# A hybrid encoder block on one core: the four activation block sums of the convolution's fifth product move into PSUM during the last z columns, and the modulation steps of the third z group begin four steps later

## The chip, the cores and the metric

The kernel runs on one core of a Trainium2 chip. Its engines are TensorE (PE in the profile; its weight loads are PEld), VectorE (DVE), ScalarE (ACT), GpSimd (POOL) and SyncE (SP), which here only issues transfers. The metric is the device time of one execution in microseconds; shown is the median of three runs.

## The reference, cut to what matters

One layer of an encoder block over 1024 tokens of width 1024, in float32: a modulation computed from a condition vector, RMSNorm, one input projection, attention, a two-way state-space branch (SSD), a gated merge and an MLP. What the change touches is the modulation and the part of the input projection that makes z and the convolution's input xBC:

```python
mod = jax.nn.silu(c) @ w_ada[l] + b_ada[l]
shift1, scale1, gate1, shift2, scale2, gate2 = [m[:, None, :] for m in jnp.split(mod, 6, axis=-1)]
h = rms_norm(x, norm1_w[l]) * (1.0 + scale1) + shift1
proj = h @ w_in[l]
q, k, v, xBC, z, dt_raw, gates = jnp.split(proj, offsets, axis=-1)
...
xBC = jax.nn.silu(depthwise_conv_centred(xBC, conv_w, conv_b))
```

## The kernel before, in words

A float32 operand is held as two pieces, a high part rounded to the type fp32r and a low part, the rest; a product is three matmuls (high x high, high x low, low x high). `split` makes the pieces: ScalarE copies the high part (line 173, a CAST in the profile), VectorE or GpSimd subtracts for the low part (through the helper `tt`, line 159). The normalised activations `h` lie transposed in SBUF as `hhi` and `hlo` (`hh` and `hl` in the profile), in 8 blocks of 128 features by two halves of 512 tokens.

**z groups.** z is made in four groups of 512 columns by `gemm_tm` (matmuls on lines 518 to 520): eight token tiles a group, each 24 matmuls into one of four PSUM banks `psq`, evicted by ScalarE with a SiLU (line 533) and stored. Each group's weights come in four pieces (`traw`), split into `twh` and `twl`. Beside the third group (`z_run(2, ...)`) runs `mod_stream`, which makes the two gate rows. Each takes eight transfers of 512 KB (`wada`, two buffers, of which the row `grow` takes one at the end), a VectorE multiply-add chain over them into `macc` (lines 224 and 226), and two matmuls with a column of ones (line 549, four rows in the profile), whose result VectorE adds to the bias. `z_run` steps a generator once per quarter of a token tile, 32 times a group; `spaced` passes every second of these on to `mod_stream`. TensorE's order in the third group is the order in which the code is written; the other engines there, and every engine in the fourth group, are put in order by a scheduler that estimates times as it builds the program. Each engine then works through its instructions strictly in that order.

Beside the fourth group (`z_run(3, ...)`) the generator `sums` makes the combinations U3, U2 and U4 of activation blocks that the convolution's products need. GpSimd adds and subtracts in tiles `df` (three buffers), ScalarE and VectorE split the results.

**The convolution's input.** xBC is made in twelve pairs of 128-column blocks, and one more pair for a gate, by Strassen-like recursion (Winograd's form): seven products (`product`, lines 919 to 921, 12 matmuls each, into four PSUM banks `psc`) in place of eight. Their activation operands are H11, H21, U2, U3, U4, H22 and the fifth, T1 = H12 - H11. `first_sum`, called in pair 0 after the second product was added, makes T1 on VectorE in SBUF tiles `u` and writes its two pieces over H12; H12 was stored to DRAM before, and is read back for the last pair. A product's weights are sums of `w_in` blocks made on GpSimd (`ws`), split by ScalarE and by VectorE or GpSimd into `wop`. Each pair's result goes through a five-tap convolution in the PSUM tile `tap` (line 863 on ScalarE, line 865 four times on VectorE, line 868 on ScalarE), and some of it is turned to token order through the PSUM tiles `pst`. tap takes two banks, pst two, psc four; they are allocated together once z's four banks are free. After the convolution come two more gate products (`psg`, line 211) and the attention.

Of the kernel before, what the change touches and what calls it, by code (L numbers as in the profile page):

```python
# [9 lines left out]
F32 = mybir.dt.float32  # L10
# [8 lines left out]
P = 128  # L19
# [72 lines left out]
def block(ctx: ExitStack, tc: tile.TileContext, ia, out, upto=99, dbg=None):  # L92
# [65 lines left out]
    def tt(e, o, a, b, op):  # L158
        e.tensor_tensor(out=o, in0=a, in1=b, op=op)  # L159
# [12 lines left out]
    def split(hi, lo, src, e_hi=None, e_lo=None):  # L172
        (e_hi or A.copy)(hi, src)  # L173
        tt(e_lo or V, lo, src, hi.bitcast(F32), ALU.subtract)
# [627 lines left out]
    with tc.tile_pool(name="p1m", bufs=1, reuse_waits="tile") as p1m, tc.tile_pool(name="ps1m", bufs=1, space=PSUM) as ps1m:  # L802

        mods = mod_stream(p1m, lambda: ps1m.tile([P, 512], F32, name="psm", tag="psm", bufs=2), 1)
        def spaced():
            for n in range(99):
                yield
                next(mods, None)
                yield

        with tc.manual_schedule(engines={mybir.EngineType.PE}):
            first = z_run(2, first, spaced(), 1)
            drain(mods)
# [3 lines left out]
    H11, H12, H21, H22 = ([(hhi[k + j][h], hlo[k + j][h]) for j in range(HK)] for k, h in ((0, 0), (0, 1), (HK, 0), (HK, 1)))  # L817
    U2, U3, U4 = ([tuple(stp.tile([P, 512], F32R, name=f"{n}{q}_{j}") for q in "hl") for j in range(HK)]
                  for n in ("u2", "u3", "u4"))
    with tc.tile_pool(name="p1b", bufs=1, reuse_waits="tile") as p1b:  # L820

        def diff(t, a, b):
            u = p1b.tile([P, 512], F32, name="df", tag="df", bufs=3)
            tt(G, t, a[0].bitcast(F32), b[0].bitcast(F32), ALU.subtract)
            tt(G, u, a[1].bitcast(F32), b[1].bitcast(F32), ALU.subtract)
            tt(G, t, t, u, ALU.add)

        def sums():

            for j in range(HK):  # L830
                t = p1b.tile([P, 512], F32, name="df", tag="df", bufs=3)
                diff(t, H22[j], H12[j])
                split(*U3[j], t)
                yield
                for q in range(2):
                    tt(G, t, t, H11[j][q].bitcast(F32), ALU.add)
                split(*U2[j], t)
                yield
                for q in range(2):
                    tt(G, t, t, H21[j][q].bitcast(F32), ALU.subtract)  # L840
                split(*U4[j], t)
                yield

        todo = sums()
        z_run(3, first, todo, 2)
        drain(todo)
        for j in range(HK):
            for q in range(2):
                dma(h12_d[q][j], H12[j][q].bitcast(F32))
# [4 lines left out]
    with tc.tile_pool(name="p2", bufs=1, reuse_waits="tile") as p2, \  # L854
# [4 lines left out]

        def conv(i, pad):  # L860

            tap = ps2.tile([P, S], F32, name="tap", tag="tap", bufs=1)
            A.activation(tap, pad[:, 0:S], AF.Identity, scale=cwT[:, i:i + 1], bias=vecT[:, CB0 + i:CB0 + i + 1])  # L863
            for k in range(1, 5):
                V.scalar_tensor_tensor(out=tap, in0=pad[:, k:k + S], scalar=cwT[:, 24 * k + i:24 * k + i + 1],  # L865
                                       in1=tap, op0=ALU.mult, op1=ALU.add)
            acc = acc_tile()
            A.activation(acc, tap, AF.Silu)
            if i >= 20:
                adma(bc_d[i - 20][:, 1], acc)  # L870
                return
            if i >= 16:
                adma(bc_d[i - 16][:, 0], acc)
            late.append(lambda: to_tokens(i, acc))
# [1 line left out]
        late = []  # L876

        def to_tokens(i, y):
            st = p2.tile([P, NT, P], F32, name="cst", tag="cst", bufs=2)
            for hf in range(2):  # L880
                pt = ps2.tile([P, 512], F32, name="pst", tag="pst", bufs=2)
                for c in range(4):
                    T.transpose(pt[:, c * P:(c + 1) * P], y[:, (hf * 4 + c) * P:(hf * 4 + c + 1) * P], ident)
                A.copy(st[:, hf * 4:hf * 4 + 4], pt.rearrange("p (c n) -> p c n", c=4))
            if i >= 16:
                adma(xb_d[i - 16][:, :, 512:640], st)
            else:
                adma(xb_d[i // 4][:, :, (i % 4) * P:(i % 4 + 1) * P], st)
# [41 lines left out]
        H0, H1 = slice(2, 514), slice(514, 1026)  # L930
        nxt = load_pair(0)

        tus = [p2.tile([P, 2, 512], F32, name="u1", tag="cst", bufs=2)]
        pre = {"ws": [p2.tile([P, HK, P], F32, name="ws", tag="ws", bufs=4)],
               "c1": [p2.tile([P, 512], F32, name="c1", tag="c1", bufs=2)],
               "p5": [p2.tile([P, 512], F32, name="p5", tag="p5", bufs=1)],
# [6 lines left out]
        def first_sum():  # L943

            for j in range(HK):
                tu = tus.pop() if tus else p2.tile([P, 2, 512], F32, name="u1", tag="cst", bufs=2)
                t, u = tu[:, 0], tu[:, 1]
                tt(V, t, H12[j][0].bitcast(F32), H11[j][0].bitcast(F32), ALU.subtract)
                tt(V, u, H12[j][1].bitcast(F32), H11[j][1].bitcast(F32), ALU.subtract)
                tt(V, t, t, u, ALU.add)  # L950
                split(*H12[j], t)

        for p, (kind, i0, _) in enumerate(pairs):
            r0, r1 = nxt
# [36 lines left out]
            done(kind, i0, pa)  # L991
        while late:
            late.pop(0)()
    sts.close()
    if upto <= 2:
        return dict( z_d=z_d, s2=s2, modc=modc)
# [1052 lines left out]
```

## Time and profile before

| what | value |
|---|---|
| median of three runs | 2447.72 us (2446.38 to 2450.83) |
| the profiled execution | 2451.32 us |
| its span, first to last instruction | 2449.5 us |
| TensorE's mean granted clock | 0.992 |
| TensorE busy, share of the span | 97% |
| HBM read, written | 250.54 MB, 113.84 MB |

In the rows of a timeline stand the start and the length in us, the engine, the line, the operation, what is written and read, and in brackets how long the engine was idle before it and what ended that. Lines are those of the kernel that was run; a helper's line stands for all its callers. Matmuls overlap: the distance between two starts, not the length of a row, is what one costs.

### The profile page before, as it was taken

What the parts mean: (1) busy time and instruction counts of PE and PEld (TensorE: products, weight loads), DVE (VectorE), ACT (ScalarE), POOL (GpSimd) and SP (SyncE); (2) the same over time, 40 slices, a digit from 0 to 9 for tenths busy, and PEclk for the clock granted to TensorE, in tenths of its full rate; (3) what the DMA queues carried; (4) which work ended last, traced back from release to release, by engine and by line L of the source; (5) the groups of instructions that cost most, each with busy time, mean ns of one, the idle gap of its engine ahead of it and who ended that gap; (6) DMA issues with size and microseconds to landing.
All of it is one profiled execution on the core that took longest, in us unless ns stands there. A gap on an engine that the chain in (4) does not pass through costs nothing.

```text
span 2449.5 us, 32244 instructions
## 1 busy us (share of the span) xinstructions
PE 2377.3 (97%) x11307; PEld 1899.4 (78%) x11307; DVE 1702.4 (69%) x2325; ACT 1091.8 (45%) x1884; POOL 827.9 (34%) x637
## 2 busy tenths in 40 slices
PE   8999999999989999999989999999999999999999
PEld 4998877888867777777767767787787888788887
DVE  5876435777756666666577796557568888768794
ACT  5455413555566666666333343344242222364430
POOL 0221107666611111110356666534006786123200
PEclk9999999999999999999999999999999999999999
DMA  7664841333531212111667765476325554654422
GB/s 255 181 184 147 259 167 65 95 104 112 185 112 52 91 52 81 57 54 48 219 205 228 221 208 176 146 270 205 132 74 194 185 197 163 234 171 138 157 79 82
DMA packets 288595, 366.53 MB, mean 150 GB/s; under 512 B 33961, under 2 KB 168849, under 8 KB 288433
## 3 DMA queue, kind: packets, MB, share of 16 engines
q1 hardware_dynamic: 216246, 288.77, 37.2%
q10 hardware_dynamic: 72187, 75.70, 9.3%
q8 instruction: 90, 1.47, 0.2%
q14 instruction: 72, 0.59, 0.1%
HBM read 250.54 MB, written 113.84 MB: 149 GB/s over the span
## 4 chain that ended last, share of the span: by engine, by line
PE 80%; DVE 8%; DMA 5%; issue 2%; ACT 2%; POOL 2%; SPq 0%; ACTq 0%; DVEq 0%; POOLq 0%
PE pst L1059 5%; PE psg L211 4%; PE psg L213 4%; PE psg L212 4%; PE p L1928 3%; PE p L1927 3%; PE p L1926 3%; PE psc L919 3%; PE psc L920 3%; PE psc L921 3%; PE psq L519 3%; PE psq L520 3%; PE psq L518 3%; PE pp L1514 3%; PE pp L1512 3%; PE pp L1513 3%
## 5 line engine op out<-in xcount | busy, mean ns | idle before, releaser
L1046 DVE TENSOR_REDUCE nm<-pss 128x1 f32<-128x1024 f32 x128 | 156.7, 1225 | 125.1 <-PE pss L1044 123.5
L1048 ACT ACTIVATE pf<-pss,nm 128x1024 f32<-128x1024 f32 x128 | 143.0, 1117 | 98.8 <-PE pst L1059 96.1
L159 DVE TENSOR_TENSOR pl<-pst,ph 128x512 fp32r<-128x512 f32 x256 | 167.6, 683 | 27.1 <-ACT ph L173 27.1
L1059 PEld LDWEIGHTS pst<-masks,pf 128*128 128x128 f32 x1024 | 117.8, 140 | 73.8 <-issue 33.9
L519 PE MATMUL psq<-twl,hh 128*128 128x512 f32 (+1 forms) x448 | 168.3, 377 | 2.5 <-DVE twl L159 2.5
L1059 PE MATMUL pst<-masks,pf 128*128 128x128 f32 x1024 | 157.4, 276 | 13.3 <-DVE pl L159 10.8
L173 ACT CAST ph<-pst 128x512 fp32r<-128x512 f32 x256 | 145.9, 586 | 54.5 <-PE pst L1059 37.9
L518 PE MATMUL psq<-twh,hh 128*128 128x512 f32 (+1 forms) x448 | 166.8, 376 | 3.5 <-ACT twh L173 3.5
L520 PE MATMUL psq<-twh,hl 128*128 128x512 f32 (+1 forms) x448 | 167.4, 375 | 0.0
L159 POOL TENSOR_TENSOR av<-av,rz 64x512 f32<-64x512 f32 x32 | 42.0, 1315 | 346.4 <-DMA rz<-rz 141.2
L1926 PE MATMUL p<-o,o 128*128 128x512 f32 x400 | 153.6, 390 | 3.3 <-ACT o L173 1.9
L1927 PE MATMUL p<-o,o 128*128 128x512 f32 x400 | 155.3, 389 | 0.2 <-DVE o L159 0.2
L1928 PE MATMUL p<-o,o 128*128 128x512 f32 x400 | 153.7, 389 | 0.0
L173 ACT CAST wop<-ws 128x512 fp32r<-128x512 f32 x116 | 71.2, 621 | 127.5 <-PE pp L1514 52.4
L865 DVE SCALAR_TENSOR_TENSOR tap<-pad,cwT,tap 128x1024 f32<-128x1024 f32 x96 | 123.4, 1285 | 4.9 <-ACT tap L863 3.5
L159 POOL TENSOR_TENSOR ws<-r,r 128x512 f32<-128x512 f32 x29 | 41.7, 1438 | 215.2 <-DVE ro L159 151.0
L159 POOL TENSOR_TENSOR sl<-sl 128x512 f32<-128x512 f32 x32 | 49.6, 1553 | 179.1 <-DVE o L159 72.7
L173 ACT CAST o<-sl 128x512 fp32r<-128x512 f32 x92 | 56.9, 622 | 104.7 <-PE p L1928 88.7
L1097 PE MATMUL pv<-pl,v 128*64 128x512 f32 x256 | 101.5, 417 | 0.0
L159 DVE TENSOR_TENSOR o<-sl,o 128x512 fp32r<-128x512 f32 x92 | 72.3, 788 | 39.8 <-ACT o L173 39.8
L211 PE MATMUL psg<-hh,whi 128*128 128x512 f32 x224 | 95.3, 425 | 1.2 <-ACT ost L1006 1.2
L518 PEld LDWEIGHTS psq<-twh,hh 128*128 128x128 f32 x448 | 84.8, 189 | 14.6 <-ACT twh L173 3.9
(457 smaller groups left out, 7026.4 us busy)
## 6 DMA issues: line engine op xcount, KB each, us to landing
ar<-r SPq DMA_DIRECT2D x100, 256.0 KB
wada<-in_w_ada_dram SPq DMA_DIRECT2D x48, 512.0 KB
r<-in_w_mlp_dram SPq DMA_DIRECT2D x32, 512.0 KB
sl<-in_w_mlp_dram SPq DMA_DIRECT2D x64, 256.0 KB
r<-in_w_in_dram SPq DMA_DIRECT2D x26, 512.0 KB
r<-ro ACTq DMA_DIRECT2D x49, 256.0 KB
r<-as SPq DMA_DIRECT2D x48, 256.0 KB
xb<-cst ACTq DMA_DIRECT2D x20, 512.0 KB
```

Source lines behind the costliest of these rows:

```text
L159: e.tensor_tensor(out=o, in0=a, in1=b, op=op)
L173: (e_hi or A.copy)(hi, src)
L211: T.matmul(ps, hi[:, k], ahi[k][half], start=k == 0, stop=False)
L518: T.matmul(o, hhi[k][half][:, sl], hi[:, k % 2, :n], start=k == 0, stop=False)
L519: T.matmul(o, hhi[k][half][:, sl], lo[:, k % 2, :n], start=False, stop=False)
L520: T.matmul(o, hlo[k][half][:, sl], hi[:, k % 2, :n], start=False, stop=k == KT - 1)
L1046: V.tensor_reduce(out=nm, in_=ps, axis=AX.X, op=ALU.max, negate=True)
L1048: A.activation(pfs[u], ps, AF.Exp, bias=nm, accum_out=zall[:, u:u + 1])
L1059: T.transpose(pt[:, k], pf[:, (hf * 4 + k) * P:(hf * 4 + k + 1) * P], ident)
L1926: T.matmul(ps, a[:, 0, sl], b[0], start=start, stop=False)
L1927: T.matmul(ps, a[:, 0, sl], b[1], start=False, stop=False)
L1928: T.matmul(ps, a[:, 1, sl], b[0], start=False, stop=stop)
```

## The change

The differences for T1 are made by a new part of `sums`, in its last four steps beside the fourth z group. Their results lie in PSUM, in banks that tap and pst use later: blocks 0 and 1 in the tap tile, 2 and 3 in two pst tiles. The second difference of each block goes through a `df` tile, and the addition writes PSUM again. `first_sum` only splits them. For that the pool of tap and pst opens before the fourth z group, so these four banks lie where the gate rows' PSUM tiles were, and psc's four come to lie on z's banks. `spaced` lets four steps of z pass first, and then passes on two of every three instead of one of two. So all 18 steps of `mod_stream` are taken within the third z group; before, 16 were, and two behind it.

```diff
--- before.py
+++ after.py
@@ -803,10 +803,13 @@
 
         mods = mod_stream(p1m, lambda: ps1m.tile([P, 512], F32, name="psm", tag="psm", bufs=2), 1)
         def spaced():
+            for n in range(4):
+                yield
             for n in range(99):
-                yield
                 next(mods, None)
                 yield
+                if n % 2:
+                    yield
 
         with tc.manual_schedule(engines={mybir.EngineType.PE}):
             first = z_run(2, first, spaced(), 1)
@@ -817,6 +820,10 @@
     H11, H12, H21, H22 = ([(hhi[k + j][h], hlo[k + j][h]) for j in range(HK)] for k, h in ((0, 0), (0, 1), (HK, 0), (HK, 1)))
     U2, U3, U4 = ([tuple(stp.tile([P, 512], F32R, name=f"{n}{q}_{j}") for q in "hl") for j in range(HK)]
                   for n in ("u2", "u3", "u4"))
+    ps2as = ExitStack()
+    ps2a = ps2as.enter_context(tc.tile_pool(name="ps2a", bufs=1, space=PSUM, reuse_waits="tile"))
+    t01 = ps2a.tile([P, S], F32, name="tap", tag="tap", bufs=1)
+    T1S = [t01[:, 0:512], t01[:, 512:S]] + [ps2a.tile([P, 512], F32, name="pst", tag="pst", bufs=2) for j in range(2)]
     with tc.tile_pool(name="p1b", bufs=1, reuse_waits="tile") as p1b:
 
         def diff(t, a, b):
@@ -840,6 +847,12 @@
                     tt(G, t, t, H21[j][q].bitcast(F32), ALU.subtract)
                 split(*U4[j], t)
                 yield
+            for j in range(HK):
+                t, u = T1S[j], p1b.tile([P, 512], F32, name="df", tag="df", bufs=3)
+                tt(V, t, H12[j][0].bitcast(F32), H11[j][0].bitcast(F32), ALU.subtract)
+                tt(V, u, H12[j][1].bitcast(F32), H11[j][1].bitcast(F32), ALU.subtract)
+                tt(V, t, t, u, ALU.add)
+                yield
 
         todo = sums()
         z_run(3, first, todo, 2)
@@ -859,7 +872,7 @@
 
         def conv(i, pad):
 
-            tap = ps2.tile([P, S], F32, name="tap", tag="tap", bufs=1)
+            tap = ps2a.tile([P, S], F32, name="tap", tag="tap", bufs=1)
             A.activation(tap, pad[:, 0:S], AF.Identity, scale=cwT[:, i:i + 1], bias=vecT[:, CB0 + i:CB0 + i + 1])
             for k in range(1, 5):
                 V.scalar_tensor_tensor(out=tap, in0=pad[:, k:k + S], scalar=cwT[:, 24 * k + i:24 * k + i + 1],
@@ -876,9 +889,9 @@
         late = []
 
         def to_tokens(i, y):
-            st = p2.tile([P, NT, P], F32, name="cst", tag="cst", bufs=2)
+            st = csts.pop() if csts else p2.tile([P, NT, P], F32, name="cst", tag="cst", bufs=2)
             for hf in range(2):
-                pt = ps2.tile([P, 512], F32, name="pst", tag="pst", bufs=2)
+                pt = ps2a.tile([P, 512], F32, name="pst", tag="pst", bufs=2)
                 for c in range(4):
                     T.transpose(pt[:, c * P:(c + 1) * P], y[:, (hf * 4 + c) * P:(hf * 4 + c + 1) * P], ident)
                 A.copy(st[:, hf * 4:hf * 4 + 4], pt.rearrange("p (c n) -> p c n", c=4))
@@ -930,7 +943,7 @@
         H0, H1 = slice(2, 514), slice(514, 1026)
         nxt = load_pair(0)
 
-        tus = [p2.tile([P, 2, 512], F32, name="u1", tag="cst", bufs=2)]
+        csts = [p2.tile([P, NT, P], F32, name="cst", tag="cst", bufs=2)]
         pre = {"ws": [p2.tile([P, HK, P], F32, name="ws", tag="ws", bufs=4)],
                "c1": [p2.tile([P, 512], F32, name="c1", tag="c1", bufs=2)],
                "p5": [p2.tile([P, 512], F32, name="p5", tag="p5", bufs=1)],
@@ -943,12 +956,7 @@
         def first_sum():
 
             for j in range(HK):
-                tu = tus.pop() if tus else p2.tile([P, 2, 512], F32, name="u1", tag="cst", bufs=2)
-                t, u = tu[:, 0], tu[:, 1]
-                tt(V, t, H12[j][0].bitcast(F32), H11[j][0].bitcast(F32), ALU.subtract)
-                tt(V, u, H12[j][1].bitcast(F32), H11[j][1].bitcast(F32), ALU.subtract)
-                tt(V, t, t, u, ALU.add)
-                split(*H12[j], t)
+                split(*H12[j], T1S[j])
 
         for p, (kind, i0, _) in enumerate(pairs):
             r0, r1 = nxt
@@ -991,6 +999,7 @@
             done(kind, i0, pa)
         while late:
             late.pop(0)()
+    ps2as.close()
     sts.close()
     if upto <= 2:
         return dict( z_d=z_d, s2=s2, modc=modc)
```

The number of instructions for the sums is the same. SyncE's order does not change. At three places the others move; the names are those of the profile, with numbers that tell the blocks apart (hh_0_345, 347, 349, 351 are the high parts of blocks 0 to 3 for the first half of the tokens, hh_1_346 to 352 for the second, and hl_ the low parts).

VectorE at the end of the fourth z group and the start of pair 0, before; `pad` is the result of a product, `wop` a weight's low half:

```order
L159 TENSOR_TENSOR u_3748<-u_3748 128x512
L159 TENSOR_TENSOR u_3819<-u_3819 128x512
L159 TENSOR_TENSOR pad<-c_3750,psc 128x512
L159 TENSOR_TENSOR wop<-r_3746,wop 128x512
L159 TENSOR_TENSOR hl_1_362<-u_3748,hh_1_346 128x512
L159 TENSOR_TENSOR hl_1_364<-u_3819,hh_1_348 128x512
L159 TENSOR_TENSOR u_3825<-hh_1_350,hh_0_349 128x512
L159 TENSOR_TENSOR u_3825<-hl_1_366,hl_0_365 128x512
L159 TENSOR_TENSOR u_3831<-hh_1_352,hh_0_351 128x512
L159 TENSOR_TENSOR u_3831<-hl_1_368,hl_0_367 128x512
L159 TENSOR_TENSOR u_3825<-u_3825 128x512
L159 TENSOR_TENSOR u_3831<-u_3831 128x512
```

And now:

```order
L159 TENSOR_TENSOR u2l_3423<-df,u2h_3422 128x512
L159 TENSOR_TENSOR df<-hl_1_368,hl_0_367 128x512
L159 TENSOR_TENSOR u4l_3437<-df,u4h_3436 128x512
L159 TENSOR_TENSOR pst<-pst,df 128x512
L159 TENSOR_TENSOR u4l_3439<-df,u4h_3438 128x512
L159 TENSOR_TENSOR hl_1_362<-tap,hh_1_346 128x512
L159 TENSOR_TENSOR hl_1_366<-pst,hh_1_350 128x512
L159 TENSOR_TENSOR hl_1_364<-tap,hh_1_348 128x512
L159 TENSOR_TENSOR hl_1_368<-pst,hh_1_352 128x512
L159 TENSOR_TENSOR pad<-c_3772,psc 128x512
L159 TENSOR_TENSOR wop<-r_3768,wop 128x512
L159 TENSOR_TENSOR pad<-c_3772,psc 128x512
```

All differences and sums stand ahead of the first `pad`, in part between the splits of U2 and U4, and the four low halves follow each other.

ScalarE at the same place, before; `zst` is z's eviction, `c` the first product's result:

```order
L534 DMA z_105<-zst 128x512
L970 COPY c_3750<-psc 128x512
L173 CAST wop<-ws 128x512
L173 CAST wop<-r_3746 128x512
L173 CAST hh_1_346<-u_3748 128x512
L173 CAST hh_1_348<-u_3819 128x512
L173 CAST wop<-ws 128x512 x3
L173 CAST hh_1_350<-u_3825 128x512
L173 CAST hh_1_352<-u_3831 128x512
L173 CAST wop<-r_3752 128x512
L173 CAST wop<-r_3873 128x512
```

And now:

```order
L534 DMA z_105<-zst 128x512
L173 CAST u4h_3438<-df 128x512
L533 ACTIVATE zst<-psq 128x512
L173 CAST hh_1_346<-tap 128x512
L534 DMA z_105<-zst 128x512
L173 CAST hh_1_350<-pst 128x512
L173 CAST hh_1_348<-tap 128x512
L173 CAST hh_1_352<-pst 128x512
L533 ACTIVATE zst<-psq 128x512
L534 DMA z_105<-zst 128x512
L978 COPY c_3772<-psc 128x512
L173 CAST wop<-ws 128x512
```

The four casts to `hh` move from among the weights' casts to behind the last U4 cast, ahead of z's last eviction.

TensorE around the second gate row (line 549), at the border of the third and fourth z groups; hh_0 belongs to the fourth group here, hh_1 to the third. Before:

```order
L518 MATMUL psq<-twh,hh_0_351 128x512
L519 MATMUL psq<-twl,hh_0_351 128x512
L520 MATMUL psq<-twh,hl_0_367 128x512
L518 MATMUL psq<-twh,hh_0_353 128x512
L549 MATMUL psm<-macc,ones 1x512 x2
L520 MATMUL psq<-twh,hl_0_363 128x512
L519 MATMUL psq<-twl,hh_0_353 128x512
L520 MATMUL psq<-twh,hl_0_369 128x512
```

And now:

```order
L518 MATMUL psq<-twh,hh_0_347 128x512
L519 MATMUL psq<-twl,hh_0_347 128x512
L520 MATMUL psq<-twh,hl_0_363 128x512
L518 MATMUL psq<-twh,hh_0_349 128x512 x3
L549 MATMUL psm<-macc,ones 1x512 x2
L518 MATMUL psq<-twh,hh_1_354 128x512
L519 MATMUL psq<-twl,hh_1_354 128x512
L520 MATMUL psq<-twh,hl_1_370 128x512
L518 MATMUL psq<-twh,hh_1_356 128x512
```

The gate row stood behind the whole third group and 18 matmuls of the fourth. It now stands behind 21 of the fourth, ahead of the last 12 of the third. The first gate row, not shown, stands six matmuls earlier than before. On VectorE the splits of the fourth group's second and third weight pieces stand behind the last multiply-add of the second gate row, where one stood ahead of it, and the split of its fourth piece behind the first three differences.

## The prediction

> **What bounds the kernel now.** I read the page first, then TensorE's waits between 283 and 430 us (the two z groups and the first convolution pair), then the timelines of each engine there. On the page TensorE is busy nearly all the span and carries the chain:
>
> ```profile
> span 2449.5 us, 32244 instructions
> PE 2377.3 (97%) x11307; PEld 1899.4 (78%) x11307; DVE 1702.4 (69%) x2325; ACT 1091.8 (45%) x1884; POOL 827.9 (34%) x637
> PE 80%; DVE 8%; DMA 5%; issue 2%; ACT 2%; POOL 2%; SPq 0%; ACTq 0%; DVEq 0%; POOLq 0%
> ```
>
> So only time in which TensorE idles or runs slowly can be won. In the stretch the change touches its waits are these (total us, times, longest):
>
> ```profile
> PE psc L919 <- ACT hh L173: 4.0, 1, 4.0
> PE psq L518 <- ACT twh L173: 3.5, 1, 3.5
> PE psq L519 <- DVE twl L159: 1.1, 2, 0.8
> PE psc L921 <- DVE wop L159: 0.4, 1, 0.4
> ```
>
> The longest is the one the change works on: the fifth product of pair 0 waits for the high half of H12's sum. TensorE around it (first matmul of the pair; its 25th; the U4 product's wait; the last before the gap and the first after it; the first at full rate again; the first of pair 1):
>
> ```profile
> 399.82 0.39 PE L919 MATMUL psc<-hh,wop 128*128 128x512 f32 x1
> 405.26 0.39 PE L919 MATMUL psc<-u2h,wop 128*128 128x512 f32 x1
> 407.53 0.50 PE L921 MATMUL psc<-u4h,wop 128*128 128x512 f32 x1 [0.36 <-DVE wop L159]
> 415.64 0.39 PE L921 MATMUL psc<-hh,wop 128*128 128x512 f32 x1
> 420.00 0.80 PE L919 MATMUL psc<-hh,wop 128*128 128x512 f32 x1 [3.97 <-ACT hh L173]
> 425.49 0.40 PE L919 MATMUL psc<-hh,wop 128*128 128x512 f32 x1
> 426.86 0.39 PE L919 MATMUL psc<-hh,wop 128*128 128x512 f32 x1
> ...
> 415.90:420.00 4.10, 0.13 (x2) 0.01 (x1) 4.02 (x5) 0.68 (x2) 2.84 (x2) 0.82 0.00 0
> 420.00:425.50 5.50, 5.50 (x13) 4.07 (x14) 4.26 (x7) 2.69 (x5) 1.09 (x2) 0.51 0.12 23
> 426.00:446.00 20.00, 20.00 (x94) 16.66 (x93) 14.97 (x16) 9.81 (x15) 12.36 (x13) 1.00 0.31 91
> 446.00:660.00 214.00, 214.00 (x1022) 178.62 (x1021) 157.33 (x165) 119.24 (x173) 134.80 (x147) 1.00 0.39 116
> ```
>
> In the last four rows the columns are the stretch, its length, the busy time of PE, PEld, DVE, ACT and POOL, the granted clock, DMA share and GB/s. After the gap the granted clock is 0.51, and from 426 to 660 TensorE is never idle, so an earlier start of pair 1 passes through the convolution whole.
>
> **The prize.** 24 matmuls go from 399.82 to 405.26, 0.227 us each. Pair 0 has seven products of 12, so 84 x 0.227 = 19.05 us at full rate; it takes 426.86 - 399.82 = 27.04. The 8.0 us lost are three pieces: the gap, 420.00 - (415.64 + 0.23) = 4.13; the 12 matmuls from 420.00 to 425.49, 5.49 instead of 2.72, 2.77; the rest, 1.1, is the start of the U2 to U4 products, which wait for ACT's and DVE's halves of the weights.
>
> The Trainium skill, "TensorE: Matmul & The Clock Gate", Part 1, says that an idle window of some 3.4 us halves the clock until a busy window has passed; the trace agrees (0.51 after 3.97 us). Two whole windows at half rate would be 3.4 us lost in place of the measured 2.77, and the prize would be 0.6 us larger by the rule; the rows decide.
>
> **Why the gap is there, and what the change does to it.** VectorE, then ScalarE, before:
>
> ```profile
> 390.31 1.12 DVE L159 TENSOR_TENSOR u2l<-df,u2h 128x512 fp32r<-128x512 f32 x1 [1.83 <-ACT u2h L173]
> 396.93 0.69 DVE L159 TENSOR_TENSOR u<-hh,hh 128x512 f32<-128x512 f32 x1
> 405.52 0.69 DVE L159 TENSOR_TENSOR pad<-c,psc 128x512 f32<-128x512 f32 x1 [4.89 <-PE psc L921]
> 407.40 3.46 DVE L159 TENSOR_TENSOR hl<-u,hh 128x512 fp32r<-128x512 f32 x2
> 410.79 1.77 DVE L159 TENSOR_TENSOR u<-hh,hh 128x512 f32<-128x512 f32 x1
> 417.54 2.35 DVE L159 TENSOR_TENSOR u<-u 128x512 f32<-128x512 f32 x2
> 404.26 1.14 ACT L173 CAST hh<-u 128x512 fp32r<-128x512 f32 x2
> 419.32 1.22 ACT L173 CAST hh<-u 128x512 fp32r<-128x512 f32 x2 [8.49 <-DVE u L159]
> ```
>
> Blocks 0 and 1 are summed at 396.9. Blocks 2 and 3 are queued behind `pad`, which waits for TensorE until 405.5, and then run at 1.77 us an instruction instead of 0.69 because POOL works at the same time. The change takes all 12 sum instructions off this place: three run before the last weight split, nine sit between the U splits, where DVE waits 1.83 us before each (the row at 390.31). ACT's four casts and DVE's four low halves then stand ahead of `pad`. Writing to PSUM costs no more: 1285 ns for `tap` in PSUM against 1.28 us for `macc` in SBUF, both 1024 columns:
>
> ```profile
> L865 DVE SCALAR_TENSOR_TENSOR tap<-pad,cwT,tap 128x1024 f32<-128x1024 f32 x96 | 123.4, 1285 | 4.9 <-ACT tap L863 3.5
> 355.99 1.28 DVE L226 SCALAR_TENSOR_TENSOR macc<-wada,sc,macc 128x1024 f32<-128x1024 f32 x1
> ```
>
> The last cast must come before about 415. Its cover is POOL's chain of U sums, which feeds the U casts ahead of it in ACT's queue:
>
> ```profile
> 388.01 1.62 POOL L159 TENSOR_TENSOR df<-df,hl 128x512 f32<-128x512 f32 x1
> 389.58 1.30 POOL L159 TENSOR_TENSOR df<-df,hh 128x512 f32<-128x512 f32 x1
> 393.90 1.61 POOL L159 TENSOR_TENSOR df<-df,hl 128x512 f32<-128x512 f32 x1
> 399.81 0.10 POOL L926 MEMSET pad<- 128x2 f32 x1 [1.22 <-PE psq L519]
> 410.28 1.73 POOL L159 TENSOR_TENSOR ws<-r,r 128x512 f32<-128x512 f32 x1
> ```
>
> The chain ends at 393.90 + 1.61 = 395.5, and POOL then waits for the end of the z matmuls until 399.81: 4.3 us of cover. Five differences with two SBUF inputs now fall into it. Lower bound: each stretches one POOL step from 1.30 to 1.62, 5 x 0.32 = 1.6 us. Upper: three differences and two additions stand ahead of the U2 split at 390.31, in an idle time of 1.83, so it comes up to 3 x 1.77 + 2 x 0.69 - 1.83 = 4.9 us late, and POOL waits for it. I take 2 us, near the lower end, since DVE idles before every other split too and can take part of them there: an end at 397.5, hidden.
>
> The Trainium skill, "SBUF — State Buffer", "Who interferes with whom", says that a VectorE instruction with two SBUF inputs contends with GpSimd's reads and the loser blocks, while one with a single SBUF input does not. The trace agrees with the first half (1.77 against 0.69). By it five blocks of 0.69 put the chain's end at 399.0, still covered, and the additions and low halves, which now have one input in PSUM, cost POOL nothing.
>
> From the end of the chain ACT needs a U cast, an eviction, four casts, an eviction, the c copy and U2's weight cast: 0.62 + 0.60 + 2.28 + 0.60 + 0.59 + 0.62 = 5.3 us (cast 0.62 or 1.14 for two, evictions as below), while U2 starts at 405.26. So the chain may end at 399.9 before TensorE feels it.
>
> **The modulation steps.** Neither SP's order nor DVE's up to the second gate changes. On TensorE the first gate row stands 6 matmuls earlier (1.4 us), the second 9 earlier (2.0 us). Before:
>
> ```profile
> 333.28 1.88 PE L549 MATMUL psm<-macc,ones 128*1 128x512 f32 x4
> 335.80 0.73 DVE L224 TENSOR_SCALAR macc<-wada,sc 128x1024 f32<-128x1024 f32 x1
> 358.43 1.88 PE L549 MATMUL psm<-macc,ones 128*1 128x512 f32 x4
> 361.85 1.27 DVE L159 TENSOR_TENSOR grow<-psm,grow 1x512 f32<-1x512 f32 x2
> 400.01 0.60 ACT L533 ACTIVATE zst<-psq 128x512 f32<-128x512 f32 x1 [3.35 <-PE psq L520]
> ```
>
> TensorE now reaches the second at 358.43 - 2.0 = 356.4, with 12 matmuls of z group 2 and all of group 3 queued behind it. Its sum was ready at 355.99 + 1.28 = 357.27. It starts over with the row after the first gate (335.80), which can come 1.4 us earlier, and the weight split in front of the last step goes behind it. If nothing of that arrives, TensorE waits 357.3 - 356.4 = 0.9 us; if all, nothing. I take 0.3. The split that now stands behind the gate is used some 10 us later.
>
> What is late next: without the gap H12's last 8 matmuls end near 415.9 + 8 x 0.227 = 417.7. H22 then needs a low half from POOL, the instruction behind the row at 410.28, so by about 410.28 + 2 x 1.73 = 413.8, and pair 1's first weights come from DVE, which has nothing else to do from 407 on. Neither is late.
>
> **Sum.** Gap 4.13 + half rate 2.77 + 0 to 0.4 of the small waits (ACT's U3 cast no longer follows two `hh` casts; I take 0) - 0.3 = 6.6 us. The profiled execution would go from 2451.3 (span 2449.5) to 2444.7; it lies 3.6 us above the median of the three runs, 2447.7, from which I take the same 6.6: **2441.1 us**.
>
> The tap and pst tiles take the lower banks, psc those of z. psc waits for z's evictions; the last of them (400.01 before, by the sum for ACT some 4 us behind POOL's end now, so 401.6) is needed by the fourth product alone, after 405.26. After the convolution, psg inherits tap's banks:
>
> ```profile
> 670.84 1.03 ACT L868 ACTIVATE cacc<-tap 128x1024 f32<-128x1024 f32 x1 [1.44 <-DVE tap L865]
> 673.53 0.39 PE L211 MATMUL psg<-hh,whi 128*128 128x512 f32 x1
> ```
>
> tap is read until 671.9, psg starts at 673.5: 1.6 us to spare, cost nothing.
>
> **The rivals.**
> - *Part is eaten* (0.19). The gate wait is 0.9, psg waits 1 to 2, or other clock drops fall differently. For it: the page's stages after 700 us wait in many places. Against: they are fed relative to TensorE. Gain 2 to 4.5, about 2444.5.
> - *POOL's chain becomes the bound* (0.08; the slower side). One mechanism: its end passes 399.9, ACT's queue holds U2's cast, TensorE stands. For it: 1.77 us contention. Against: 4.3 us of cover. At 404 TensorE stands 4.1 us and the half rate, 2.8, returns: nothing won. Past that it loses; at 407, 7.1 + 2.8 - 6.9 = 3 us, about 2451.
> - *The stall moves* (0.07). The sums are early, but the next operand (H22's weight low half, or pair 1's) is as late. For it: POOL is packed from 405 on. Against: POOL sums pair 1 at 410.28, over 9 us ahead of pair 1's new start near 420. Gain 0 to 2, about 2446.7.
> - *The forecast* (0.66): 2439 to 2443.
>
> **How the numbers follow.** About 0.2% (4.9 us) is what a measurement of this kernel can tell from no change. The forecast passes it in nearly all its range, the first rival seldom: faster 0.67. Same, from the rest of these and the third: 0.26; slower, nearly all POOL's: 0.07. Range: low 2447.7 - 8.2 (no wait at the gate, the small waits gone, 1 us of scatter) less a little, 2438.5; high 2446.5, which takes in the first rival.
>
> **What would show it.** Right: no `hh` wait before the fifth product, casts of `hh` near 398 to 400, clock 1.0 from 416 to 426, pair 1 near 420. Wrong: POOL's last `df` after 400, a TensorE wait over 1 us at L549's second row, or a wait before psg or in pair 1.

## The result, and the profile after

The changed kernel takes 2438.41 us, median of 8 runs (2436.52 to 2442.18), beside 2447.32 us for the kernel before on the same chip. The ratio is 0.9964, 95% interval 0.9954 to 0.9973, that is 8.9 us less where 6.6 were forecast. A second comparison on another occasion gave 0.9953 (0.9941 to 0.9966), 11.5 us less. The profiled execution of the changed kernel took 2441.72 us, with a span of 2439.9. The convolution's lines stand 13 later than before (L919 is L932), those of the attention 9 later (L1046 is L1055).

TensorE's waits between 283 and 430 us after the change (total us, times, longest), and two rows of the view by stretches, in the columns the prediction explains:

```profile
PE psq L518 <- ACT twh L173: 2.8, 1, 2.8
PE psq L519 <- DVE twl L159: 0.5, 1, 0.5
PE psc L934 <- DVE wop L159: 0.3, 1, 0.3
PE psm L549 <- DVE macc L226: 0.3, 1, 0.3
...
416.00:426.00 10.00, 10.00 (x46) 8.29 (x45) 7.00 (x8) 4.26 (x7) 5.80 (x5) 1.00 0.18 55
446.00:660.00 214.00, 214.00 (x1017) 178.55 (x1016) 157.65 (x166) 118.90 (x172) 132.60 (x142) 1.00 0.41 125
```

The 4.0 us for `hh` are gone, and from 416 to 426 TensorE is busy throughout at a clock of 1.00, where before it had 0.51 from 420.0 to 425.5. The timelines of the changed kernel around the seam (POOL, ACT, then PE: the second gate row, the first product, the first matmul of pair 1):

```profile
388.16 1.29 POOL L159 TENSOR_TENSOR df<-df,hh 128x512 f32<-128x512 f32 x1 [1.24 <-DVE u3l L159]
395.77 1.68 POOL L159 TENSOR_TENSOR df<-df,hh 128x512 f32<-128x512 f32 x1 [0.63 <-DVE u2l L159]
397.53 1.62 POOL L159 TENSOR_TENSOR df<-df,hl 128x512 f32<-128x512 f32 x1
399.19 0.62 ACT L173 CAST u4h<-df 128x512 fp32r<-128x512 f32 x1 [2.89 <-POOL df L159]
400.20 0.58 ACT L173 CAST hh<-tap 128x512 fp32r<-128x512 f32 x1
402.03 0.59 ACT L173 CAST hh<-pst 128x512 fp32r<-128x512 f32 x1
357.31 1.88 PE L549 MATMUL psm<-macc,ones 128*1 128x512 f32 x4 [0.30 <-DVE macc L226]
400.73 0.39 PE L932 MATMUL psc<-hh,wop 128*128 128x512 f32 x1
420.41 0.39 PE L932 MATMUL psc<-hh,wop 128*128 128x512 f32 x1
```

Pair 0 now takes 420.41 - 400.73 = 19.68 us instead of 27.04. So far the result is the one that was forecast. But the convolution is not all. These are the waits of TensorE for `pl` at the start of the attention, with the first and the ninth maximum of the scores on VectorE, before:

```profile
PE pst L1059 <- DVE pl L159: 4.0, 3, 1.6
...
681.74 1.23 DVE L1046 TENSOR_REDUCE nm<-pss 128x1 f32<-128x1024 f32 x1 [7.24 <-PE pss L1044]
706.98 1.22 DVE L1046 TENSOR_REDUCE nm<-pss 128x1 f32<-128x1024 f32 x1 [0.77 <-PE pss L1044]
```

and after:

```profile
PE pst L1068 <- DVE pl L159: 0.5, 1, 0.5
...
675.28 1.22 DVE L1055 TENSOR_REDUCE nm<-pss 128x1 f32<-128x1024 f32 x1 [7.24 <-PE pss L1053]
696.18 1.23 DVE L1055 TENSOR_REDUCE nm<-pss 128x1 f32<-128x1024 f32 x1 [0.77 <-PE pss L1053]
```

Eight units of the attention (a unit is one tile of 128 tokens of one head) take 696.18 - 675.28 = 20.90 us instead of 706.98 - 681.74 = 25.24, though no line of that stage was edited. From ScalarE's timeline, before and then after, the first rows there:

```profile
684.58 1.12 ACT L1048 ACTIVATE pf<-pss,nm 128x1024 f32<-128x1024 f32 x1 [0.38 <-DVE nm L1046]
685.92 0.59 ACT L173 CAST ph<-pst 128x512 fp32r<-128x512 f32 x1
687.11 1.12 ACT L1048 ACTIVATE pf<-pss,nm 128x1024 f32<-128x1024 f32 x1 [0.60 <-PE pst L1059]
688.21 1.06 ACT L173 CAST ph<-pst 128x512 fp32r<-128x512 f32 x2
693.52 0.63 PE L1059 MATMUL pst<-masks,pf 128*128 128x128 f32 x4 [1.57 <-DVE pl L159]
```

```profile
678.12 1.11 ACT L1057 ACTIVATE pf<-pss,nm 128x1024 f32<-128x1024 f32 x1 [0.38 <-DVE nm L1055]
679.46 0.59 ACT L173 CAST ph<-pst 128x512 fp32r<-128x512 f32 x1
680.59 0.59 ACT L173 CAST ph<-pst 128x512 fp32r<-128x512 f32 x1 [0.54 <-PE pst L1068]
681.08 1.12 ACT L1057 ACTIVATE pf<-pss,nm 128x1024 f32<-128x1024 f32 x1
```

Before, the third exponential (`pf`) stands ahead of the second cast (`ph`) of the first unit; after, behind it. VectorE's order moves with it: the low half of that cast (`pl`) comes behind the fourth maximum before (689.12 behind 687.98), and ahead of it after (681.21 ahead of 681.82). Counted from the first maximum, that cast starts 688.21 - 681.74 = 6.47 us in before, and 5.31 after. The low half `pl` is the last reader of the transposes' buffer, and TensorE waits for it three times, 1.57 us in the row shown. Between the two maxima these waits are 4.0 us before and none after; the 0.5 in the row after comes later.

The two stages can be measured apart in every kernel: from the start of the first product to the start of the first maximum (before: 681.74 - 399.82 = 281.92), and from the first maximum to the ninth. All kernels that follow, in us:

| kernel | first product to first maximum | first to ninth maximum | ratio to before (95%) |
|---|---|---|---|
| before | 281.92 | 25.24 | 1 |
| the change | 274.55 | 20.90 | 0.9964 (0.9954 to 0.9973) |
| the change again | 274.53 | 20.91 | 0.9953 (0.9941 to 0.9966) |
| sums alone | 276.11 | 20.90 | 0.9966 (0.9954 to 0.9978) |
| steps alone | 281.73 | 25.26 | 0.9999 (0.9991 to 1.0008) |
| banks alone | 281.69 | 25.22 | 0.9998 (0.9989 to 1.0006) |
| no sums at all | 274.53 | 20.89 | 0.9955 (0.9943 to 0.9967) |
| attention's order alone | 281.75 | 20.89 | 0.998 (0.997 to 0.999) |
| GpSimd 4 sums longer | 279.15 | 20.91 | 0.998 (0.9969 to 0.9991) |
| GpSimd 2 sums longer | 276.17 | 20.92 | 0.9959 (0.9945 to 0.9972) |
| loads later | 275.05 | 25.23 | 0.9964 (0.9951 to 0.9978) |
| loads later, attention's order | 275.05 | 20.90 | 0.9954 (0.9942 to 0.9967) |

By stages the change saves 7.4 + 4.3 = 11.7 us. That lies just outside the first comparison (0.9973 to 0.9954 is 6.6 to 11.3 us) and inside the second. Stages that repeat agree to 0.25 us, and from the ninth maximum to the last all twelve profiles take 460.9 to 461.3 us. But from the last maximum, near 1160 us, to the end they scatter between 1278.6 and 1283.3 us, and the start of the first product between 397.75 and 400.73, so one time alone cannot tell apart kernels that differ by 2 us, and the stages can.

### The profile page after: what moved, and what is told of

Its sections match the earlier page's. It is cut to its first block, busy times and chain, and to the rows that moved or that the text cites. A ratio compares the mean times of both kernels' runs of the same rounds, so it can differ in the third digit from the quotient of the medians.

```text
span 2439.9 us, 32245 instructions
## 1 busy us (share of the span) xinstructions
PE 2377.0 (97%) x11307; PEld 1900.4 (78%) x11307; DVE 1699.4 (70%) x2325; ACT 1092.2 (45%) x1884; POOL 828.8 (34%) x637
## 5 line engine op out<-in xcount | busy, mean ns | idle before, releaser
L1055 DVE TENSOR_REDUCE nm<-pss 128x1 f32<-128x1024 f32 x128 | 156.7, 1225 | 120.3 <-PE pss L1053 118.7
```

Source lines behind the costliest of these rows:

```text
L1055: V.tensor_reduce(out=nm, in_=ps, axis=AX.X, op=ALU.max, negate=True)
```

## The experiments

**The parts of the change.** Sums in PSUM with the old spacing of the modulation steps, against the changed kernel:

```
-            for n in range(4):
-                yield
             for n in range(99):
+                yield
                 next(mods, None)
                 yield
-                if n % 2:
-                    yield
```

> The change with the old spacing of the modulation steps (one step in every second of the z group's turns, from the first turn). My theory: the sums made early in PSUM carry the whole gain and the steps carry none of it. In the convolution's first pair the wait of TensorE for the split block sums (3.97 us before) and the half-rate stretch behind it (2.77 us) are both gone, the rows of the attention's first units stand in the order of the changed kernel, and the time is within 1.5 us of the changed kernel: 2437 to 2440 us, 0.9955 to 0.997 of before. Rival (the steps are what lets the sums finish early): VectorE reaches the first sum later, part of the wait returns, and the time is 2441 to 2445 us.

Measured: 2441.61 us, 0.9966. By the ratio this is the time of the theory, though 2441.61 us itself lies outside its 2437 to 2440: the kernel before took 2450.11 us beside it. The theory is also right on the attention and on the `hh` wait, which stays away. The rival is right on the mechanism: a wait returns, 1.56 us of the stage, but a different one. First TensorE's waits in this kernel (283 to 430 us), then the start of the U lows on VectorE, the end of GpSimd's chain, the cast behind it and the first product:

```profile
PE psc L929 <- ACT wop L173: 1.7, 2, 1.3
...
363.33 0.70 DVE L159 TENSOR_TENSOR tap<-hh,hh 128x512 f32<-128x512 f32 x1
365.15 1.28 DVE L159 TENSOR_TENSOR u3l<-df,u3h 128x512 fp32r<-128x512 f32 x2
398.99 1.62 POOL L159 TENSOR_TENSOR df<-df,hl 128x512 f32<-128x512 f32 x1
400.64 0.62 ACT L173 CAST u4h<-df 128x512 fp32r<-128x512 f32 x1 [3.38 <-POOL df L159]
399.35 0.39 PE L929 MATMUL psc<-hh,wop 128*128 128x512 f32 x1
```

GpSimd's chain ends at 400.61, 1.26 us behind the first product; with the change it ended at 399.15, 1.58 ahead. The cause stands on VectorE. In the changed kernel:

```profile
360.74 0.70 DVE L159 TENSOR_TENSOR tap<-hh,hh 128x512 f32<-128x512 f32 x1
362.98 1.23 DVE L159 TENSOR_TENSOR twl<-traw,twh 128x1024 fp32r<-128x1024 f32 x1 [0.33 <-ACT twh L173]
364.12 1.28 DVE L159 TENSOR_TENSOR u3l<-df,u3h 128x512 fp32r<-128x512 f32 x2
```

With the new steps the gate's two rows are done before the last weight split, and the first three sums run while VectorE waits for that split's high half, an idle time that shrinks to 0.33 us. With the old steps the same sums stand behind the split, and the lows of U3, on which GpSimd's chain hangs, come 399.35 - 365.15 = 34.2 us ahead of the first product instead of 36.6. That is 2.4 of the 2.8 us by which the chain ends later. So the steps are what keeps the chain early.

The other half, the steps alone in the kernel before:

```
+            for n in range(4):
+                yield
             for n in range(99):
-                yield
                 next(mods, None)
                 yield
+                if n % 2:
+                    yield
```

> The kernel before with the new spacing of the modulation steps alone; the sums stay in the convolution. My theory: nothing but the 0.3 us wait of the gate's rows, so 2447 to 2448 us, same as before; the 3.97 us wait and the half-rate stretch stay. Rival (the steps carry part of the gain): 2443 to 2446 us.

Measured: 2449.88 us, 0.9999. Both waits that the change removes are there (4.0 us for `hh`; 25.26 us for the eight units). The steps win nothing without the sums.

The new pool alone, in the kernel before:

```
+    ps2as = ExitStack()
+    ps2a = ps2as.enter_context(tc.tile_pool(name="ps2a", bufs=1, space=PSUM, ...))
     with tc.tile_pool(name="p1b", bufs=1, reuse_waits="tile") as p1b:
...
-            tap = ps2.tile([P, S], F32, name="tap", tag="tap", bufs=1)
+            tap = ps2a.tile([P, S], F32, name="tap", tag="tap", bufs=1)
...
-                pt = ps2.tile([P, 512], F32, name="pst", tag="pst", bufs=2)
+                pt = ps2a.tile([P, 512], F32, name="pst", tag="pst", bufs=2)
...
+    ps2as.close()
```

> The kernel before with the new pool of PSUM alone: the banks of tap and pst are taken before the last z group and kept to the convolution's end, but the block sums stay in SBUF, after the start of the convolution. Every engine's rows stand in the order of the kernel before. My theory (the order of the attention's rows makes its 4.4 us, the early sums make the convolution's 7.4 us, the banks make nothing): same as before, 0.999 to 1.001, the wait of 4 us for the split sums stays, and the attention's first eight units take 25.2 us as before. Rival (the attention gains because its tiles inherit other banks): those units take 20.9 us and the ratio is 0.998.

Measured: 2449.08 us, 0.9998. Its waits, from the two stretches:

```profile
PE psc L921 <- ACT hh L173: 4.0, 1, 4.0
...
PE pst L1062 <- DVE pl L159: 4.0, 3, 1.6
```

The banks make neither gain; the rival falls.

**The limit.** The kernel before without the first sums; the fifth product is then made from the plain block, so this kernel's result is not the layer's, and only its time counts:

```
-            if p == 0:
-                first_sum()
```

> The kernel before with the call of the first sums left out: the fifth product of the first pairs is then made from the plain second block, so 12 sums, 4 casts and 4 low parts are not computed at all, and no PSUM bank is moved. This is the upper bound of what the change can take. My theory: the wait of 3.97 us and the 2.77 us of half rate are gone, and the attention's rows stand in the changed kernel's order, so 6.9 + 4.4 = 11.3 us less than before, 2436 us (2435 to 2438); the changed kernel's 2438.4 then leaves no more than 2.5 us behind. Rival (the stall is not what the time hung on, or the gain in the attention is of the banks): 2440 to 2443 us.

Measured: 2439.47 us, 0.9955, 11.0 us less. The convolution's stage takes 274.53 us, what the changed kernel needs with all the sums made. In that stage the change leaves nothing behind. The attention gains here too, with no bank moved and no instruction added.

**The attention.** In the kernel before, only the exponential of the third unit is written later:

```
                 if u + 2 < NU:
-                    scores(u + 2)
+                    scores(u + 2, u in (0,))    # True: keeps its exponential back
                     yield 0.92
...
                         if c:
                             yield c
+                    elif exps:
+                        exps.pop()()
```

> The kernel before with one thing moved in the attention: the exponential of the third unit is written behind the first unit's second turn, which gives ScalarE and VectorE the row order that the changed kernel has there; the convolution is untouched. My theory: the 4.4 us that the changed kernel gains between the attention's first score and its eighth come from this order alone, so 2443 us (0.9982 of before, 2442 to 2444.5), and the three waits of TensorE for pl in the attention's first 30 us are gone. Rival (those 4.4 us are jitter of one run, or belong to the PSUM banks that the attention's tiles inherit): within 1 us of before, 2446.5 to 2448.

Measured: 2443.74 us, 0.998. The eight units take 20.89 us, and TensorE's waits for `pl` in that stretch are gone; the convolution keeps its 281.75. The order of a few rows alone makes the attention's gain. The edit moves both the cast ahead of the exponential and its low half ahead of the maximum; the two were not tried apart. The same from the other side came with the loads of pair 0 held back in the changed kernel:

```
                 split(*U3[j], t)
+                if j == 0:
+                    for h in range(2):
+                        rp.append(wp.tile([P, HK, 2, P], F32, name="r0", tag="wraw"))
+                        V.tensor_copy(rp[h][:, 0, 0, 0:1], U3[0][1][:, 0:1].bitcast(F32))
                 yield
...
-                t = p2_tile("r1", [P, HK, 2, P], 1) if h and p else wp.tile(...)
+                t = p2_tile("r1", [P, HK, 2, P], 1) if h and p else rp.pop(0) if p == 0 else wp.tile(...)
```

> The changed kernel with the two weight loads of the convolution's first pair held back until the first low part of U3 is made, some 75 us later (each tile is first touched by a copy of one column from it). In the last z groups their 1 MB then no longer runs ahead of the weights for which TensorE waits 2.8 us (3.5 before). By this move the attention's first rows on ScalarE and VectorE stand in the order of the kernel before again, while the early sums stay. So it separates the two gains from the other side. My theory: from first product to first score 274.6 us as with the change; the attention's first eight units 25.2 us as before, 4.35 us more; in the z group 1 to 3 us less; together 0.995 to 0.997 of before. Rival (the attention's gain hangs on the sums, not on the order): 20.9 us for the eight units and 0.9935 to 0.995.

Measured: 2441.26 us, 0.9964. The wait row of this kernel at the attention's start:

```profile
PE pst L1074 <- DVE pl L159: 4.5, 4, 1.6
```

The sums are early, the convolution's stage takes 275.05, and the eight units take 25.23 again. The rival falls: the attention's gain does not hang on the sums. With the exponential written later as well:

> The same with the attention's exponential of the third unit written behind the first unit's second turn, so that the rows there stand as in the changed kernel. My theory: both gains of the change (7.4 us in the convolution, 4.35 us in the attention) and 1 to 6 us in the z group, by how much of the wait of 2.8 us and of the half-rate stretch behind it goes: 2433 to 2438 us, 0.9930 to 0.9950 of before, faster than the changed kernel. Rival (the wait in the z group is set by the transfers of the modulation's weights and not by these loads, or the casts come back as a wait at the convolution's start): no less than the changed kernel, 0.9950 to 0.9965.

Measured: 2437.07 us, 0.9954, no faster than the changed kernel by these intervals, so the rival holds and the theory's 0.9930 to 0.9950 does not. The wait for `twh` in the z group falls to 1.2 us from 2.8. In exchange the convolution's stage is 0.5 us longer, with 0.6 us of waits for `wop` where the change has 0.3. The first product starts at 397.75 and 398.16 us in the two kernels with later loads, in the other ten profiles between 398.29 and 400.73: what the loads are worth in the z group is not told apart from that scatter. The order is worth the 4.3 us whatever stands ahead of it.

**The cover on GpSimd.** Two or four more sums at the end of the chain:

```
                     tt(G, t, t, H21[j][q].bitcast(F32), ALU.subtract)
+                if j == HK - 1:
+                    for op in (ALU.add, ALU.subtract) * 2:      # * 1 for two
+                        tt(G, t, t, H21[j][0].bitcast(F32), op)
                 split(*U4[j], t)
```

> The same with two more sums instead of four; the cast of the last U sum keeps its place on ScalarE ahead of the split sums' casts. GpSimd's chain ends 2 x 1.45 = 2.9 us later, 1.3 us behind the convolution's first product, as it did with the old spacing of the steps (1.46 us behind it, where the stage from first product to first score took 276.1 us, 1.56 us more than with the change). My theory (the cast at the head of the queue): the same 1.5 us, 276 us for the stage, TensorE waits 1 to 2 us for a weight cast of ScalarE, no half clock; 0.9955 to 0.9975 of before. Rival (the 1.56 us of the old spacing come from VectorE's modulation steps and not from GpSimd's end): 274.6 us, no wait for a weight cast.

Measured: 2439.72 us, 0.9959; the stage takes 276.17 us, 1.63 more than with the change. The end of the chain and the first product:

```profile
398.67 2.66 POOL L159 TENSOR_TENSOR df<-df,hh 128x512 f32<-128x512 f32 x2
399.85 0.39 PE L935 MATMUL psc<-hh,wop 128*128 128x512 f32 x1
```

The chain ends 401.33 - 399.85 = 1.48 us behind the first product. By another way than the old steps the same lateness has the same price (1.26 us behind cost 1.56), and a wait of the same kind, 1.7 us for a weight cast. It is GpSimd's end, not the steps as such, that decides.

> The changed kernel with four more sums on GpSimd behind the last U sum (the same block added and taken away twice, values as before up to rounding). GpSimd's chain, which ended 1.6 us ahead of the convolution's first product, then ends some 4 x 1.45 = 5.8 us later, 4.2 us behind it. With this length the last cast of a U sum stands four rows later on ScalarE, behind the last eviction of the z group and the casts of the split sums. My theory: what hurts is not the late chain but a cast that waits for it at the head of ScalarE's queue; with the cast moved back, the first products get their operands, and from first product to first score it takes no more than 1 us over the changed kernel's 274.6 us, 0.996 to 0.9975 of before. Rival (the prediction's second rival: the chain itself becomes the bound): TensorE waits 4 us, the clock falls to half rate behind it as it did before, 281 us for this stage, and the whole gain there is gone, 0.998 to 0.9995.

Measured: 2444.84 us, 0.998; the stage takes 279.15 us, 4.6 more than with the change. TensorE and ScalarE around it, and the granted clock by stretches:

```profile
399.11 5.39 POOL L159 TENSOR_TENSOR df<-df,hh 128x512 f32<-128x512 f32 x4
400.24 0.39 PE L935 MATMUL psc<-hh,wop 128*128 128x512 f32 x1
404.53 0.62 ACT L173 CAST u4h<-df 128x512 fp32r<-128x512 f32 x1 [4.34 <-POOL df L159]
408.25 0.50 PE L935 MATMUL psc<-u2h,wop 128*128 128x512 f32 x1 [2.41 <-ACT wop L173]
409.49 0.50 PE L935 MATMUL psc<-u3h,wop 128*128 128x512 f32 x1 [0.50 <-ACT wop L173]
...
410.30:413.80 3.50, 3.50 (x10) 2.53 (x9) 0.27 (x1) 0.00 (x0) 3.50 (x3) 0.52 0.83 241
413.80:416.00 2.20, 2.20 (x11) 1.80 (x10) 0.00 (x0) 0.62 (x1) 2.17 (x3) 1.00 0.21 74
```

My theory falls: with the cast moved back four rows it still cost 4.6 us and not 1. The cast waits for GpSimd's end at 404.50, and behind it on ScalarE stand the last z eviction, the copy of c1 and U2's weight cast, and U2's product waits 2.41 us. The last z eviction, which the expectation had put ahead of the cast, stayed behind it. The rival has the mechanism, with a smaller price than it said (279.15 and not 281): TensorE idles 2.9 us, and 3.5 us at a clock of 0.52 cost another 1.7.

The changed kernel once more, beside the banks alone and the two longer chains:

> The changed kernel once more, beside the kernel before on the same chip. By the stages of the traces so far the change saves 7.4 us between the first product of the convolution and the first score (the sums early in PSUM with the new steps), and 4.4 us in the attention's first eight units, 11.7 us in all, 0.9952 of before; the first comparison had 0.9964 (0.9954 to 0.9973). If all that the stages show arrives at the end, this run gives 0.9945 to 0.996; if about 2 us of it are lost again behind the attention, 0.996 to 0.9975.

Measured: 2438.5 us, 0.9953. Its stages repeat those of the first profile to 0.02 us, its GpSimd chain ends 1.22 us ahead of the first product, and what the stages show arrives at the end. The first half of the expectation holds, though 0.9964 lies inside this interval too.

## Why the prediction was right, and where it was not

- **The prize: right.** 8.0 us was read as lost in pair 0. Without any sums the stage is 7.4 us shorter, and the change takes all of that.
- **Gap and half rate, 6.9: right.** Both are gone. **The small waits: mis-sized.** The prediction took 0 of 0 to 0.4; the stage gained 7.37, which leaves 7.37 - 6.90 = 0.47 for them. Of the 1.1 us lost before, the wait list shows 0.3 for `wop` now.
- **Sums in PSUM cost no more, and fit between the U splits: right.** The differences with two SBUF inputs took 1.77, 1.77, 0.93 and 0.68 us there, the additions into PSUM 0.69 or 0.70.
- **GpSimd's chain, 2 us later: mis-sized, inside its bounds.** Against the first product it moved from 4.31 us ahead to 1.58, and to 1.22 in the second profile: 2.7 to 3.1 us, between the 1.6 and 4.9 given. It waits for lows of VectorE (1.24 and 0.63 in the rows above), as the upper bound said, and some of its sums are stretched (the one at 395.77 took 1.68 us, its like before 1.29 or 1.30), as the lower one did. So the `hh` casts came at 400.2 to 402.6, not 398 to 400; they were needed by about 415.
- **The point from which it is felt: right to 0.4 us.** 399.9 was 0.1 us behind the first product. The two chains that ended 1.26 and 1.48 us behind it cost 1.56 and 1.63 us; taken one for one, the point lies 0.15 to 0.3 ahead of it. With the chain's end 1.58 and 1.22 us ahead, the change has some 0.9 to 1.4 us left, not the 2.4 that the prediction's 397.5 gave.
- **Its second rival** was sized as 4.1 + 2.8 for an end at 404. An end at 404.50 cost 4.6 us in all. The half rate did return, for a shorter time. It is not quite the case that was priced: the four `hh` casts, 2.28 us of the prediction's list, stood ahead of the late cast there.
- **The wait at the gate, 0.3: right** (0.30). **But the part on the steps missed what they are for.** It counted them as 0.3 us of loss. It noted that three sums run before the last weight split, but gave that place no price. There they let the three sums run in an idle time; without that GpSimd ends 2.84 us later and 1.56 us of the gain go.
- **What is late next, the banks behind the convolution, the full stretch from 446 to 660: right.** TensorE waits for none of them, and its wait for psg at the attention's start is 0.7 us on ScalarE's eviction, as before.
- **The failed step: that the sum ends with the convolution.** Its only look behind the convolution was at the banks that psg inherits, "1.6 us to spare, cost nothing". The order of ScalarE's and VectorE's rows at the start of the attention changes too, and that is 4.3 of the 11.7 us. The order alone brings it in the old kernel, and goes without it in the new one; the banks do nothing.

The forecast of 2441.1 was 2.7 us too slow. The measured saving of 8.9 us lies just inside the range, whose low end is 9.2 us under 2447.7; the 11.7 us of the stages and the 11.5 of the second comparison lie outside it. So the mechanism in the convolution was the right one with nearly the right size, 7.4 us for 6.6. But 4.3 us were missing from the sum, and that the time still falls at the edge of the range is luck of the scatter.

What stays open is why these rows came out in another order. They did when the first sums left the convolution, with banks moved or not, and stood as before when two loads were held back as well; the order is fixed when the kernel is built, and which earlier time decides it was not traced. Nor was it measured how the scatter behind the attention splits among its stages.

## What to carry to other kernels

When work is moved and the order of the rows is made by a scheduler, compare the rows of every later stage, not only those around the edit: here a third of the gain came some 270 us behind it, from a cast that no longer stands behind an exponential and its low half that no longer stands behind a maximum, and holding back two loads lost it again. To know what a cover is worth, express its end against the first instruction that needs it, and lengthen it by known amounts: here two delays of much the same length, made in different ways, had much the same price. Where runs scatter by more than the effect, measure stages between two rows of the trace.

## What was not expected of the hardware

The clock halves after waits far shorter than the 3.97 us of before. In the kernel with four sums more, waits of 2.41 and 0.50 us within 3.7 us are followed by 3.5 us at 0.52. In the kernel with the old steps, at the start of a z group, two waits of under 1 us do it; in the kernel with later loads two waits nearly as long don't:

```profile
309.32 0.49 PE L518 MATMUL psq<-twh,hh 128*128 128x512 f32 x1 [0.93 <-ACT twh L173]
310.58 0.50 PE L519 MATMUL psq<-twl,hh 128*128 128x512 f32 x1 [0.77 <-DVE twl L159]
311.20:314.60 3.40, 3.40 (x10) 2.63 (x9) 2.50 (x3) 1.61 (x2) 0.00 (x0) 0.51 0.94 288
```

```profile
309.56 0.50 PE L518 MATMUL psq<-twh,hh 128*128 128x512 f32 x1 [0.73 <-ACT twh L173]
310.82 0.50 PE L519 MATMUL psq<-twl,hh 128*128 128x512 f32 x1 [0.76 <-DVE twl L159]
312.00:316.00 4.00, 4.00 (x20) 3.29 (x19) 3.42 (x3) 0.60 (x1) 0.00 (x0) 1.00 0.94 305
```

The Trainium skill, "TensorE: Matmul & The Clock Gate", Part 1, says that the clock falls after at least one idle window of about 3.4 us, and that the windows run freely. The length of the half rate agrees with it (3.4 and 3.5 us here); that the window must be idle, taken as idle throughout, does not agree with waits of 0.93 and 0.77 us. In the convolution of the kernel with the old steps, waits of 1.35 and 0.30 us leave the clock at 1.00, nearly as much idle time in all. Where the bound lies, or whether it is the phase, these runs don't tell.

Nor does one length of wait give one length of half rate. Before, the gap in front of the fifth product is followed by 12 matmuls in 5.49 us (420.00 to 425.49). With the banks alone the gap is as long, and full rate is back after 9:

```profile
419.29 0.50 PE L921 MATMUL psc<-hh,wop 128*128 128x512 f32 x1 [3.97 <-ACT hh L173]
423.47 0.39 PE L921 MATMUL psc<-hh,wop 128*128 128x512 f32 x1
```

Read in stretches of half a microsecond, the granted clock before is down from 418.5 to about 425.2 us, so its fall lies 1.5 us ahead of the gap's end. With the banks alone it is down from about 419.9 to 423.3, half as long, and falls 0.6 us after the gap. What follows the gap costs 2.77 us in the one profile and 4.18 - 9 x 0.227 = 2.1 in the other, 0.22 of it a short wait for `hl`. The stage still takes the same time to 0.25 us, because in the second profile another wait of 0.5 us, for a weight's cast, stands ahead of the gap. So the price of a stall of 4.0 us was 6.9 us in one profile and 6.3 in another, and a forecast from one profile carries that spread.
